# Seven down products summed in three pairs of PSUM banks, and two token tiles stored from GpSimd's queue

## The chip, the cores and the metric

One core of one Trainium2 chip runs the kernel. The metric is the device time of one execution in microseconds; the kernel before took 1035.12 us, the median of three runs (1033.83 to 1036.23).

## The reference, cut to what matters

One decoder layer on 512 tokens of width 1024: two token mixers, a layer norm, a gated feed-forward part, and a second layer norm whose result is the output. Only the last step is touched here:

```python
def swiglu(x, w_gate, w_up, w_down):
    return (jax.nn.silu(x @ w_gate) * (x @ w_up)) @ w_down
...
ff = swiglu(h, w_ffn_gate[l], w_ffn_up[l], w_ffn_down[l])
h = layer_norm(DEEPNORM_ALPHA * h + ff, ln2_g[l], ln2_b[l])
```

All of it is float32. `w_down` is 2816 x 1024.

## The kernel before, in words

**The down product.** The product of the 512 x 2816 activations with the 2816 x 1024 weights is made with seven products of half-size blocks in place of eight (Winograd's form of Strassen's scheme): tokens in two halves of 256, the inner dimension in two halves of 1408 (11 blocks of 128), the columns in two halves of 512. Their left sides are the activation blocks `a11`, `a12`, `a22` and the combinations `s1` to `s4`, which VectorE (DVE) forms while the feed-forward products run; their right sides are `w_down`'s own blocks or combinations of them that were written to the DRAM buffer `td` earlier, through GpSimd's (POOL's) DMA queue (`combine_weights`, L1085 to L1097).

**One product** (loop at L1207). It walks six weight blocks (five of 128 x 1024 values, one of 128 x 512). For each, `load_w` (L164) issues a load on SyncE's (SP's) queue into one of three buffers `wr`; `split_w` (L173) makes a high part `wh` by a cast on ScalarE (ACT, L135) and a low part `wl` by a subtraction on DVE (L121), each with three buffers; `mm3` (L154) then issues three matmuls (high x high, high x low, low x high) for each 128 rows. The load goes on when the subtraction of three blocks earlier has freed its `wr`. While product q runs, `left` (L1173) splits the left side of product q+1 in the same way, on ACT and DVE. One product is 11 blocks x 2 token tiles (`i` = 0, 1) x 3 = 66 matmuls of 512 columns.

**Where results gather.** Each half product sits in a PSUM bank of 128 x 512. Once a product is complete, `Norm.add` (L992) adds the bank to the rows `h1` in SBUF on DVE: a scalar_tensor_tensor (L124), and, where the sum of that half row is then complete, a bn_stats (L998). In the kernel before, three pairs of banks take the products as: `c11` a11 then a12 on top; `cx` s2 then s3 on top; `cy` s1 then s4 on top; a22 has banks of its own (`dl`). The product a11 belongs to three sums of four, so `first_sum` reads its bank three times for each token tile. Names in the trace: `dc` is c11, `dx` is cx, `dy` is cy.

**The last product, a22** (`final`), keeps the split weights of blocks 3 to 5 in buffers of their own, runs all of token tile 2 through before tile 3 for them, and cuts tile 3's 512 columns into two groups of 256.

**The layer norm and the stores.** `Norm.finish` (L1000) makes mean and scale from the statistics in eight small DVE instructions and one ACT square root. For tiles 0, 1 and 2 the row is then scaled on ACT and multiplied and added to on POOL (four instructions of 128 x 512 a tile); for tile 3 (`fast`) two DVE instructions a half do all. Tiles 0 and 1 are finished behind s4, the fifth product; tiles 2 and 3 behind a22, the seventh. Each finished tile is stored in two halves of 256 KB by DMAs that are issued from SP's queue:

```python
if last and (final or name == "s4"):
    t = i if name == "s4" else 2 + i
    lns[t].finish(t == 3)
    for jj in range(2):
        nc.sync.dma_start(out=out[0, t * P:(t + 1) * P, T * jj:T * jj + T], in_=h1[t][:, jj])
```

**What sets the order.** TensorE's (PE's) instructions run in the order of the program text. The other engines and queues are put in order by the scheduler at build time; each then runs its own list strictly in that order, so an instruction that waits holds those behind it on the same engine or queue.

Of the kernel before, what the change touches and what calls it, by code (L numbers as in the profile page):

```python
# [30 lines left out]
ALPHA = 2.0 ** 0.25  # L31
LN_EPS = 1e-5
RMS_EPS = 1e-6
P = 128
T = 512
# [11 lines left out]
def layer_kernel(  # L47
# [7 lines left out]
    nc = tc.nc  # L55
    ctx.enter_context(tc.manual_schedule(engines={mybir.EngineType.PE}))
    V, S, G, PE = nc.vector, nc.scalar, nc.gpsimd, nc.tensor
# [13 lines left out]
    def slot(name, dt=F32):  # L71
        if not line:
            raise RuntimeError(f"no slot for {name}")
        tag = line.pop(0)
        t = big.tile([P, 2, T], dt, tag=tag, name=name)
        held[id(t)] = (t, tag)
        return t

    def free(*tiles):
        for t in tiles:  # L80
            line.append(held.pop(id(t))[1])
# [3 lines left out]
    def bank(ring, name):  # L85
        tag = rings[ring].pop(0)
        rings[ring].append(tag)
        return pp.tile([P, T], F32, tag=tag, name=name)

    def bankp(name):  # L90
        return bank("p", name)

    def bankd(name):
        return bank("d", name)
# [19 lines left out]
    def flat(t):  # L114
        return t.rearrange("p a b -> p (a b)")
# [38 lines left out]
    def mm3(ps, wh, wl, rh, rl, start, stop, **kw):  # L154
        PE.matmul(ps, wh, rh, start=start, stop=False, **kw)  # L155
        PE.matmul(ps, wh, rl, start=False, stop=False, **kw)  # L156
        PE.matmul(ps, wl, rh, start=False, stop=stop, **kw)  # L157
# [6 lines left out]
    def load_w(src, raw=None):  # L164

        wcount[0] += 1
        if raw is None:
            raw = wp.tile([P, 1024], F32, tag="wr", bufs=3, name=f"wr{wcount[0]}")
        v = view_w(raw, *src.shape[1:])
        nc.sync.dma_start(out=v, in_=src)  # L170
        return v

    def split_w(raw, eng=None, hi=None, lo=None):  # L173

        wcount[0] += 1
        if hi is None:
            hi = wp.tile([P, 1024], F32R, tag="wh", name=f"wh{wcount[0]}")
        if lo is None:
            lo = wp.tile([P, 1024], F32R, tag="wl", name=f"wl{wcount[0]}")
        n = raw.shape[1] * raw.shape[2]  # L180
        split_flat(hi[:, :n], lo[:, :n], raw.rearrange("p a b -> p (a b)"), eng)
        return view_w(hi, *raw.shape[1:]), view_w(lo, *raw.shape[1:])
# [211 lines left out]
    for b in range(4):  # L394
        G.tensor_copy(out=eye32[32 * b:32 * b + 32],
                      in_=ident[32 * b:32 * b + 32, 32 * b:32 * b + 32])
# [474 lines left out]
    for n in range(4 * NK):  # L871

        k, i = (n // 4, n % 4) if n < 24 else (6 + n % 2, (n - 24) // 2)
# [150 lines left out]
    h1 = []  # L1024
    for i in range(4):
        t = slot(f"h1{i}")
# [4 lines left out]
    lns = [Norm(h1[i], g1, b1, f"ln1{i}") for i in range(4)]  # L1031
# [23 lines left out]
    for i in range(4):  # L1055
        ps = bankp(f"mx1_{i}")
# [22 lines left out]
    a11 = []  # L1079
# [83 lines left out]
    lns = [Norm(h1[i], g2, b2, f"ln2{i}", 4 if i == 3 else 2) for i in range(4)]  # L1163

    def rows_of_weights(i, c):
        return lambda p, n: wd[:, 2 * p + i:2 * p + i + 2 * n - 1:2, T * c:T * c + T]

    def combined(c):
        return lambda p, n: td[p:p + n, :, T * c:T * c + T].rearrange("k p c -> p k c")
# [3 lines left out]
    def left(n, p, m):  # L1173

        t = slot(f"{n}{p}", F32R)
        split(t[:, 0, 0:256 * m], t[:, 1, 0:256 * m], flat(parts[n][p // 4])[:, 256 * (p % 4):256 * (p % 4 + m)])
        if p % 4 == 2 or p + m == NP:
            free(parts[n][p // 4])
        return t

    c11 = [bankp(f"dc{i}") for i in range(2)]
    cx = [bankp(f"dx{i}") for i in range(2)]
    cy = [bankd(f"dy{i}") for i in range(2)]

    def first_sum(i, ps):
        for ln, c in ((lns[i], T), (lns[2 + i], 0), (lns[2 + i], T)):
            ln.add(ps, c, last=False)

    def onto(lo, i0, **kw):
        return lambda i, ps: lns[i0 + i].add(ps, lo, **kw)  # L1190

    def p7_done(i, ps):
        lns[2 + i].add(ps, T, 1.0)
        lns[2 + i].add(ps, 0, 1.0, False)


    products = [
        ("a11", rows_of_weights(0, 0), c11, True, first_sum),
        ("s2", combined(3), cx, True, onto(T, 0, alpha=1.0, last=False)),
        ("s1", combined(0), cy, True, onto(T, 2, alpha=1.0, last=False)),  # L1200
        ("a12", rows_of_weights(1, 0), c11, False, onto(0, 0)),
        ("s4", rows_of_weights(1, 1), cy, False, onto(T, 0, alpha=1.0)),
        ("s3", combined(1), cx, False, p7_done),
        ("a22", combined(2), None, True, onto(0, 2, alpha=1.0)),
    ]
    ready = a11
    for q, (name, right, banks, new, then) in enumerate(products):  # L1207
        lhs, ready = ready, []
        final = q == 6
        tops = [[(0, b)] for b in banks] if not final else [  # L1210
            [(0, bankp("dl0"))], [(0, bankp("dl1")[:, 0:256]), (256, bankd("dl2")[:, 0:256])]]
        pend = []
        for m, (p, n) in enumerate(blocks):
            keep = final and m >= 3
            extra = [flat(slot(f"wd{m}{e}", F32R)) if keep else None for e in range(2)]
            pend.append((m, n, *split_w(load_w(right(p, n)), None, *extra)))
            if not final:
                ready.append(left(products[q + 1][0], p, n))
            if keep and m < 5:
                continue  # L1220
            last = m == len(blocks) - 1
            for i in range(2):
                for c, ps in tops[i]:
                    w = ps.shape[1]
                    for mm, nn, wh, wl in pend:
                        for k in range(nn):
                            ts = slice(256 * k + P * i, 256 * k + P * i + P)
                            mm3(ps, lhs[mm][:, 0, ts], lhs[mm][:, 1, ts], wh[:, k, c:c + w], wl[:, k, c:c + w],
                                new and mm == k == 0, last and mm == m and k == nn - 1,
                                **({} if new else dict(skip_group_check=True)))  # L1230
                    if last:
                        if final:
                            lns[2 + i].add(ps, c, 1.0)
                        else:
                            then(i, ps)
                if last and (final or name == "s4"):
                    t = i if name == "s4" else 2 + i
                    lns[t].finish(t == 3)
                    for jj in range(2):
                        nc.sync.dma_start(out=out[0, t * P:(t + 1) * P, T * jj:T * jj + T], in_=h1[t][:, jj])  # L1240
            pend = []
        free(*lhs)

# [23 lines left out]
```

## Time and profile before

| | us |
|---|---|
| median of three runs | 1035.12 |
| the profiled execution | 1030.49 |
| its span, first to last instruction | 1028.8 |
| around the span | 1.7 |
| PE busy | 987.4 |
| DVE busy | 622.8 |
| ACT busy | 453.2 |
| POOL busy | 274.3 |

The span is what the rows below divide; times in them are microseconds from its start. The seven products take its last eighth, from 898.6 on. A busy PE is not a PE at its peak, since its clock can be granted at half; the row of the granted clock says when. Idle time before an instruction stands in brackets in a timeline, with what ended it.

### The profile page before, as it was taken

The numbers are of one execution on the slowest core, as the hardware profiler recorded it, in microseconds if no ns is written. First come the engines' busy times: TensorE is split into PE (matmuls) and PEld (weight loads), VectorE is DVE, ScalarE is ACT, GpSimd is POOL, SyncE is SP. The second block draws the span as 40 slices with busy tenths as digits, with TensorE's granted clock in tenths as the row PEclk, the third lists the DMA queues.
The fourth block names the chain that finished last, engine by engine and source line by source line (L and its number), as shares of the span: only waits on it lengthen the run. The fifth ranks groups of instructions, "written<-read, shape, count | busy, mean of one in ns | idle before, by whom it ended". The sixth has DMA issues, their size and how long they took to land.

```text
span 1028.8 us, 14366 instructions
## 1 busy us (share of the span) xinstructions
PE 987.4 (96%) x5531; PEld 811.6 (79%) x5531; DVE 622.8 (61%) x1321; ACT 453.2 (44%) x621; POOL 274.3 (27%) x278
## 2 busy tenths in 40 slices
PE   7999989999999999999999999999999999999974
PEld 4887767877887888788888888898788888878864
DVE  3769989837777872264333555957543334597565
ACT  5589463368326643764311333322222222465432
POOL 2372624516332723274100003232100000000052
PEclk9999999999999999999999999999999999999996
DMA  8332223223222323153334337489833333346551
GB/s 252 108 99 55 80 73 83 63 72 82 63 62 73 90 65 92 42 145 111 102 97 151 101 122 207 178 298 376 283 92 103 103 92 113 103 143 204 195 162 64
DMA packets 161544, 128.52 MB, mean 125 GB/s; under 512 B 5499, under 2 KB 140860, under 8 KB 161476
## 3 DMA queue, kind: packets, MB, share of 16 engines
q1 hardware_dynamic: 152608, 100.17, 33.1%
q0 software_dynamic: 7552, 27.27, 7.3%
q8 instruction: 43, 0.70, 0.3%
q10 hardware_dynamic: 1316, 0.16, 0.1%
q14 instruction: 25, 0.20, 0.1%
HBM read 113.94 MB, written 13.65 MB: 124 GB/s over the span
## 4 chain that ended last, share of the span: by engine, by line
PE 56%; issue 16%; DVE 14%; DMA 5%; ACT 4%; POOL 4%; SPq 0%; DVEq 0%; ACTq 0%; POOLq 0%
PE pj L155 3%; DMA b<-in_w_ffn_down 3%; PE pj L157 3%; PE pj L156 3%; PE g L155 3%; PE g L157 3%; PE g L156 3%; DVE xa L121 3%; PE fu L155 2%; PE fu L156 2%; PE fu L157 2%; PE fg L157 2%; PE fg L155 2%; PE fg L156 2%; PE yl L157 2%
## 5 line engine op out<-in xcount | busy, mean ns | idle before, releaser
L135 ACT CAST wh<-wr 128x1024 fp32r<-128x1024 f32 (+1 forms) x163 | 168.5, 1034 | 374.2 <-PE fg L156 78.0
L121 POOL TENSOR_TENSOR wl<-wr,wh 128x512 fp32r<-128x512 f32 x128 | 172.6, 1371 | 216.2 <-ACT wh L135 212.9
L121 DVE TENSOR_TENSOR wl<-wr,wh 128x1024 fp32r<-128x1024 f32 x99 | 117.9, 1193 | 131.9 <-ACT wh L135 131.8
L155 PE MATMUL pj<-xT,wh 128*128 128x512 f32 x224 | 92.6, 413 | 0.0
L157 PE MATMUL pj<-xT,wl 128*128 128x512 f32 x224 | 88.0, 393 | 0.0
L156 PE MATMUL pj<-xT,wh 128*128 128x512 f32 x224 | 87.9, 392 | 0.0
L127 ACT ACT_TABLE_LOAD x62 | 79.5, 1283 | 12.8 <-DMA rw<-in_lru_conv_w 7.2
L157 PE MATMUL fg<-hk,wl 128*128 128x512 f32 x160 | 62.4, 390 | 0.5 <-DVE wl L121 0.5
L155 PE MATMUL fg<-hk,wh 128*128 128x512 f32 x160 | 62.3, 389 | 0.0
L156 PE MATMUL fg<-hk,wh 128*128 128x512 f32 x160 | 62.3, 389 | 0.0
L155 PE MATMUL fu<-hk,wh 128*128 128x512 f32 x160 | 62.2, 389 | 0.0
L156 PE MATMUL fu<-hk,wh 128*128 128x512 f32 x160 | 62.2, 389 | 0.0
L157 PE MATMUL fu<-hk,wl 128*128 128x512 f32 x160 | 62.2, 389 | 0.0
L155 PE MATMUL g<-xT,wh 128*128 128x512 f32 x128 | 51.1, 399 | 0.0
L124 DVE SCALAR_TENSOR_TENSOR x<-pj,cols,x 128x511 f32<-128x511 f32 (+2 forms) x60 | 44.5, 742 | 9.7 <-ACT x L127 9.3
L157 PE MATMUL g<-xT,wl 128*128 128x512 f32 x128 | 50.0, 391 | 0.0
L156 PE MATMUL g<-xT,wh 128*128 128x512 f32 x128 | 49.9, 390 | 0.0
L157 PEld LDWEIGHTS pj<-xT,wl 128*128 128x128 f32 x224 | 42.3, 189 | 9.2
L155 PEld LDWEIGHTS pj<-xT,wh 128*128 128x128 f32 x224 | 42.5, 190 | 7.9
L121 POOL TENSOR_TENSOR h<-h,g 128x512 f32<-128x512 f32 x6 | 10.0, 1664 | 145.4 <-ACT h L127 145.4
L156 PEld LDWEIGHTS pj<-xT,wh 128*128 128x128 f32 x224 | 42.6, 190 | 7.3
L121 DVE TENSOR_TENSOR xa<-xa 128x16 f32<-128x16 f32 (+14 forms) x116 | 37.6, 324 | 2.3
(380 smaller groups left out, 2370.6 us busy)
## 6 DMA issues: line engine op xcount, KB each, us to landing
wr<-in_w_in SPq DMA_DIRECT2D x64, 512.0 KB, 3.7
wr<-in_w_ffn_gate SPq DMA_DIRECT2D x22, 512.0 KB, 3.6
wr<-in_w_ffn_up SPq DMA_DIRECT2D x22, 512.0 KB, 3.6
b<-in_w_ffn_down POOLq DMA_DIRECT2D x22, 512.0 KB, 5.8
td<-b POOLq DMA_DIRECT2D x22, 512.0 KB, 4.6
wr<-td SPq DMA_DIRECT2D x20, 512.0 KB, 3.9
wr<-in_w_ffn_down SPq DMA_DIRECT2D x15, 512.0 KB, 3.3
wr<-in_w_branch_lru SPq DMA_DIRECT2D x8, 512.0 KB, 3.5
```

What stands on the lines that cost most here:

```text
L121: return eng.tensor_tensor(out=o, in0=a, in1=b, op=op)
L124: return V.scalar_tensor_tensor(out=o, in0=a, scalar=s, in1=b, op0=op0, op1=op1)
L127: return S.activation(out=o, in_=i, func=func, **kw)
L135: S.copy(out=hi, in_=src)
L155: PE.matmul(ps, wh, rh, start=start, stop=False, **kw)
L156: PE.matmul(ps, wh, rl, start=False, stop=False, **kw)
L157: PE.matmul(ps, wl, rh, start=False, stop=stop, **kw)
```

## The change

Three pairs of banks are kept, now `ca`, `cb`, `cc`. a11, s2, s3 and, for the first token tile, a22 are gathered one on top of the other in `ca`, which is read in between (after a11 for columns 0 to 511 of tiles 0 and 1, after s2 for columns 512 to 1023 of these, after s3 for tiles 2 and 3); s1 and s4 share `cb`; a12 has `cc`. The order of s1 and s2, and that of s3 and s4, are exchanged, so s4, behind which tiles 0 and 1 are finished, is now the sixth product and not the fifth. The stores of tiles 0 and 1 are issued from POOL's queue; those of tiles 2 and 3 stay on SP's.

```diff
@@ -1178,37 +1178,37 @@
             free(parts[n][p // 4])
         return t
 
-    c11 = [bankp(f"dc{i}") for i in range(2)]
-    cx = [bankp(f"dx{i}") for i in range(2)]
-    cy = [bankd(f"dy{i}") for i in range(2)]
-
-    def first_sum(i, ps):
-        for ln, c in ((lns[i], T), (lns[2 + i], 0), (lns[2 + i], T)):
-            ln.add(ps, c, last=False)
+
+    ca = [bankp(f"da{i}") for i in range(2)]
+    cb = [bankd(f"db{i}") for i in range(2)]
+    cc = [bankp(f"dc{i}") for i in range(2)]
 
     def onto(lo, i0, **kw):
         return lambda i, ps: lns[i0 + i].add(ps, lo, **kw)
 
     def p7_done(i, ps):
         lns[2 + i].add(ps, T, 1.0)
-        lns[2 + i].add(ps, 0, 1.0, False)
+        if i == 1:
+            lns[3].add(ps, 0, last=False)
 
 
     products = [
-        ("a11", rows_of_weights(0, 0), c11, True, first_sum),
-        ("s2", combined(3), cx, True, onto(T, 0, alpha=1.0, last=False)),
-        ("s1", combined(0), cy, True, onto(T, 2, alpha=1.0, last=False)),
-        ("a12", rows_of_weights(1, 0), c11, False, onto(0, 0)),
-        ("s4", rows_of_weights(1, 1), cy, False, onto(T, 0, alpha=1.0)),
-        ("s3", combined(1), cx, False, p7_done),
-        ("a22", combined(2), None, True, onto(0, 2, alpha=1.0)),
+        ("a11", rows_of_weights(0, 0), ca, True, onto(0, 0, last=False)),
+        ("s1", combined(0), cb, True, onto(T, 2, last=False)),
+        ("s2", combined(3), ca, False, onto(T, 0, last=False)),
+        ("a12", rows_of_weights(1, 0), cc, True, onto(0, 0, alpha=1.0)),
+        ("s3", combined(1), ca, False, p7_done),
+        ("s4", rows_of_weights(1, 1), cb, False, onto(T, 0, alpha=1.0)),
+        ("a22", combined(2), ca, False, None),
     ]
     ready = a11
     for q, (name, right, banks, new, then) in enumerate(products):
         lhs, ready = ready, []
         final = q == 6
-        tops = [[(0, b)] for b in banks] if not final else [
-            [(0, bankp("dl0"))], [(0, bankp("dl1")[:, 0:256]), (256, bankd("dl2")[:, 0:256])]]
+        tops = [[(0, b, new)] for b in banks]
+        if final:
+
+            tops[1] = [(0, bankd("dl1")[:, 0:256], True), (256, bankd("dl2")[:, 0:256], True)]
         pend = []
         for m, (p, n) in enumerate(blocks):
             keep = final and m >= 3
@@ -1220,24 +1220,25 @@
                 continue
             last = m == len(blocks) - 1
             for i in range(2):
-                for c, ps in tops[i]:
+                for c, ps, fresh in tops[i]:
                     w = ps.shape[1]
                     for mm, nn, wh, wl in pend:
                         for k in range(nn):
                             ts = slice(256 * k + P * i, 256 * k + P * i + P)
                             mm3(ps, lhs[mm][:, 0, ts], lhs[mm][:, 1, ts], wh[:, k, c:c + w], wl[:, k, c:c + w],
-                                new and mm == k == 0, last and mm == m and k == nn - 1,
-                                **({} if new else dict(skip_group_check=True)))
+                                fresh and mm == k == 0, last and mm == m and k == nn - 1,
+                                **({} if fresh else dict(skip_group_check=True)))
                     if last:
                         if final:
-                            lns[2 + i].add(ps, c, 1.0)
+                            lns[2 + i].add(ps, c, 1.0 if i else ALPHA)
                         else:
                             then(i, ps)
                 if last and (final or name == "s4"):
                     t = i if name == "s4" else 2 + i
                     lns[t].finish(t == 3)
                     for jj in range(2):
-                        nc.sync.dma_start(out=out[0, t * P:(t + 1) * P, T * jj:T * jj + T], in_=h1[t][:, jj])
+                        (nc.sync if final else G).dma_start(out=out[0, t * P:(t + 1) * P, T * jj:T * jj + T],
+                                                            in_=h1[t][:, jj])
             pend = []
         free(*lhs)
```

## Rows read from the trace of the kernel before

**Rows 1.** The page: busy time, share of the span, instructions
```profile
PE 987.4 (96%) x5531; PEld 811.6 (79%) x5531; DVE 622.8 (61%) x1321; ACT 453.2 (44%) x621; POOL 274.3 (27%) x278
```

**Rows 2.** Busy time by stretch: sixth product, seventh, the slow part of that
```profile
core 0: us, PE busy (x) PEld busy (x) DVE busy (x) ACT busy (x) POOL busy (x), PEclk, DMA share, GB/s
975.90:990.90 15.00, 15.00 (x67) 12.41 (x67) 12.41 (x25) 10.31 (x13) 7.48 (x5) 1.00 0.55 183
990.90:1017.10 26.20, 18.42 (x99) 15.69 (x97) 11.85 (x26) 4.38 (x6) 5.46 (x4) 0.87 0.30 91
...
1005.00:1009.60 4.60, 4.38 (x15) 3.92 (x16) 3.16 (x4) 1.74 (x3) 0.00 (x0) 0.51 0.22 59
```

**Rows 3.** Timeline of PE: start, duration, instruction [idle before, what ended it]
```profile
898.58 0.39 PE L155 MATMUL dc<-wh,a 128*128 128x512 f32 x1
...
918.70 0.50 PE L156 MATMUL dx<-wl,s 128*128 128x512 f32 x1 [2.05 <-DVE wl L121]
...
975.73 0.39 PE L155 MATMUL dx<-wh,s 128*128 128x512 f32 x1
...
990.69 0.39 PE L155 MATMUL dl<-wh,a 128*128 128x512 f32 x1
...
995.43 0.50 PE L156 MATMUL dl<-wl,a 128*128 128x512 f32 x1 [1.56 <-DVE wl L121]
...
1003.96 0.80 PE L155 MATMUL dl<-wh,a 128*128 128x512 f32 x1 [5.67 <-ACT wh L135]
...
1013.26 0.28 PE L155 MATMUL dl<-wd,a 128*128 128x256 f32 x1
...
1016.73 0.28 PE L157 MATMUL dl<-wd,a 128*128 128x256 f32 x1
```

**Rows 4.** Timeline of SP's queue, then its waits (us in total, times, longest)
```profile
966.19 17.91 SPq L170 DMA_DIRECT2D wr<-td  x8
986.27 10.61 SPq L1240 DMA_DIRECT2D out<-h  x4
996.98 8.55 SPq L170 DMA_DIRECT2D wr<-td  x4
...
SPq L1240 <- POOL h L121: 28.8, 6, 14.9
```

**Rows 5.** Timeline of DVE, around the second product's start and at 986
```profile
913.71 3.80 DVE L124 SCALAR_TENSOR_TENSOR h<-h,dc 128x512 f32<-128x512 f32 x8
917.43 3.49 DVE L121 TENSOR_TENSOR wl<-wr,wh 128x1024 fp32r<-128x1024 f32 x3
...
986.18 0.68 DVE L121 TENSOR_TENSOR wl<-wr,wh 128x512 fp32r<-128x512 f32 x1
```

**Rows 6.** Groups by form, 898 to 1029: one read of a full bank
```profile
L124 DVE SCALAR_TENSOR_TENSOR h<-h,dc 128x512 f32<-128x512 f32 x6 | 3.8, 681 | 1.1 <-PE dc L157 1.1
```

**Rows 7.** Timeline of POOL: tiles 0 and 1 (first, slowest, last), then tile 2
```profile
983.26 1.61 POOL L121 TENSOR_TENSOR h<-h,g 128x512 f32<-128x512 f32 x1 [124.32 <-ACT h L127]
...
989.35 2.28 POOL L121 TENSOR_TENSOR h<-h,g 128x512 f32<-128x512 f32 x1
...
994.33 2.19 POOL L121 TENSOR_TENSOR h<-h,b 128x512 f32<-128x512 f32 x1
1017.57 1.27 POOL L121 TENSOR_TENSOR h<-h,g 128x512 f32<-128x512 f32 x1 [21.05 <-ACT h L127]
...
1022.25 1.26 POOL L121 TENSOR_TENSOR h<-h,b 128x512 f32<-128x512 f32 x1
```

**Rows 8.** Groups of POOL by line: DMA issues, count, busy, mean ns
```profile
L1096 POOL DMA_DIRECT2D td<-b x22 | 11.8, 536 | 50.5 <-DVE b L121 38.5 <-DVE hk L121 11.0 <-PE f L157 0.9
```

**Rows 9.** DMA issues: count, KB each, median us from issue to landing
```profile
td<-b POOLq DMA_DIRECT2D x22, 512.0 KB, 4.6
...
out<-h SPq DMA_DIRECT2D x8, 256.0 KB, 2.3
```

**Rows 10.** Timeline of SP's queue: the last store
```profile
1024.75 0.33 SPq L1240 DMA_DIRECT2D out<-h  x1
```

## What the change does to the time: a prediction

> **What bounds the kernel now.** I read the page first: PE is busy for 96% of the span [rows 1], so time can come only from places where PE stands still or runs slowly, and from the end behind its last matmul. Next comes the table of stretches over the seven products. The sixth product takes 15.0 us at a granted clock of 1.00; the seventh, a22, with as many multiplications, takes 26.2 us, and DVE, ACT and POOL are all less than half busy in it [rows 2]. So none of them is short of time there: something is late.
>
> The timeline of PE says what. One product takes 990.69 - 975.73 = 14.96 us, which is 66 matmuls at 0.2267 us. In a22, PE stands for 1.56 us and then for 5.67 us [rows 3], and after the long stop its granted clock is 0.51, the 1.2 GHz level, from 1005.0 to 1009.6 [rows 2]. The 256-column matmuls follow each other every 0.12 us (29 steps from 1013.26 to 1016.73 [rows 3]). An unhindered a22 has 33 matmuls of 512 columns and 66 of 256, 33 x 0.2267 + 66 x 0.12 = 15.4 us, so 10.9 us are lost there.
>
> SP's queue gives the cause. Eight loads (six of s3, two of a22) are issued, then come the four stores of tiles 0 and 1, from 986.27 to 996.88, and only behind them a22's other four loads, at 996.98 [rows 4]. The stores wait for POOL's layer norm (14.9 us in the longest wait [rows 4]), which works from 983.26 to 996.52 [rows 7]. The buffer for the first held load was free at 986.86, when the low part of the block before was done [rows 5]: the queue and not the buffer held it, for 10 us.
>
> The other places: PE stood 2.05 us at the second product [rows 3], since DVE made 3.80 us of bank reads (`first_sum`) before the three low parts that were due [rows 5]. And 11.8 us lie between PE's last matmul (1016.73 + 0.28 = 1017.0) and the end: the layer norms of tiles 2 and 3, and the last stores.
>
> **The change, part by part.**
>
> *Stores of tiles 0 and 1 leave SP's queue.* Nothing that waits for POOL now stands ahead of a22's loads. These go back to waiting for their buffers, as the loads of the sixth product did, which ran without a stop [rows 2]. Taken: the whole 10.9 us. The other end is that the last blocks are wanted sooner (below, the third rival).
>
> *The reads.* Counting a full bank as one, twenty reads become fifteen: after a11 two in place of six, after s3 three in place of four. At 0.68 us each [rows 6] this is 3.4 us of DVE, beside PE's work except at the second product. There 3.80 - 2 x 0.68 = 2.4 us go from in front of the due low parts, more than the 2.05 us stall: PE gains 2.05 us, at the least 0, if another piece of work is put in the gap.
>
> *Waits that the banks add.* s2 may write `ca` only after a11's reads, s3 after s2's, a22 after s3's: a whole other product of 14.96 us lies between each pair, so they cost nothing; without it PE would stand for the two reads, 1.4 us. One is closer. The ring `d` has three banks left, so the second half of tile 3 in a22 writes the bank of `cb` that s4's read leaves. That read is due some 0.7 us before a22 starts (tile 0's matmuls end three before s4's last), and the matmuls that want it come 6 x 0.2267 + 6 x 0.12 = 2.1 us after the start. Taken: nothing; at most the 1.56 us of the stall now seen at that place.
>
> *s4 becomes the sixth product.* PE's own timeline: 898.58 + 6 x 14.96 = 988.34 for the end of s4, and 988.34 + 15.4 + 0.16 = 1003.9 for PE's last matmul to end, 13.1 us sooner than 1017.0. If the 11.8 us behind it stayed, the span would be 1015.7.
>
> They do not stay. Tiles 0 and 1 are now finished during a22, and POOL does this and then tile 2. In the kernel before, POOL's first instruction starts 983.26 - 975.73 = 7.53 us behind s4 [rows 3, 7], and its eight take 13.26 us; tile 2's four, much later, take 5.94 us [rows 7]. Now POOL starts at 988.34 + 7.53 = 995.9 and is not done with tiles 0 and 1 when tile 2 is ready: tile 2's rows reach POOL in the kernel before 1017.57 - 1013.26 = 4.3 us behind the last of its matmuls [rows 3, 7], now at 988.34 + 11.8 + 4.3 = 1004.4. Behind POOL's instructions for tiles 0 and 1 stand the moved stores as well.
>
> *The four stores on POOL's queue.* The nearest rows are the stores to `td` from the same queue, 0.536 us of POOL each [rows 8], so 2.1 us. At the other end they cost POOL what the slowest instruction beside DVE was stretched by, 2.28 - 1.26 = 1.0 us each more [rows 7], 6.2 us in all. I take 2.1, since the rows are of the same operation. Landing takes 4.6 us for twice the bytes there, against 2.3 on SP's queue [rows 9]; tile 1's stores go out 5.5 us or more before tile 2 is done, which covers it.
>
> *The sum.* POOL's instructions of 128 x 512 take 1.26 us alone and up to 2.28 us while DVE works [rows 7]. Tiles 0 and 1: 8 x 1.27 = 10.2 to 13.26 us; tile 2: 5.1 to 5.94. DVE has fewer low parts to make during a22's second half and is done near 1011.6, so I take the middle of each: 12.5 + 2.1 + 5.5 = 20.1 us from 995.9, POOL done at 1016.0. Behind it three stores go from SP's queue, 0.33 us each, and from the end of the last of them to the end of the span it is 1028.8 - 1025.08 = 3.7 us [rows 10]: 4.7 us together. Span 1020.7, so 8.1 us less than 1028.8. By the ends of these terms POOL is done between 1013.3 and 1017.2, or 1.56 us later with the stall above: 5.3 to 10.8 us less. (With the stores at 6.2 us as well, every term at its worst, it would be 1.2 us less.)
>
> The profiled execution took 1030.49 us, 1.69 around its span, and lies 4.6 below the median of 1035.12. I put the difference on the median: 1035.12 - 8.1 = 1027.0, own range 1024.3 to 1029.8.
>
> **The rivals.**
>
> *POOL keeps up.* If tiles 0 and 1 are done before tile 2 arrives, DVE's tile 3 sets the end: span 1015.7, time 1022.0. For it: PE's gain of 13.1 us is real. Against it: POOL would have to be done with all twelve instructions and four stores by 1015.7 - 4.7 = 1011.0, 15.1 us after it starts, where the quickest rows give 10.2 + 2.1 + 5.1 = 17.4. Only an earlier start, or POOL's list in another order, does it.
>
> *The stores are held while DVE works.* Then tile 1's two stores go out only as DVE ends, 7.7 us behind PE's last matmul [rows 3, 10], at 1011.6; two stores and tile 2 follow, 1.1 + 5.5, and the 4.7: span 1022.9, time 1029.2. Against it, 22 stores were issued from POOL at a mean of 0.536 us [rows 8] while DVE was forming the combinations that they store. The Trainium skill ("SBUF — State Buffer", "SBUF: two separate sides") names this as a trap: a DMA from GpSimd's queue needs its descriptors written by GpSimd, which certain two-port DVE instructions lock out, and it advises SP's or ACT's queue, which speaks against this change; the rows of 0.536 us do not show it, and no row tells whether DVE's instructions behind a22 are of that kind. By the figures of the page's next section ("A bandwidth-pool intuition that's wrong"), 3.1 us in place of 0.62 for a DMA, four stores would add 4 x 2.5 = 9.9 us, an estimate from that page, and the time would be 1036.9.
>
> *a22 still starves.* PE takes blocks 3 to 5 of tile 2 in a row (6 x 0.2267 = 1.4 us each), and those of tile 3 after them, so block 4 is wanted 1.4 us and block 5 2.8 us sooner than with tile by tile in turn, while DVE and ACT make the layer norm of tiles 0 and 1 in between. For it: low parts behind bank reads stopped PE for 1.56 us. Against it: the same mix ran in the sixth product without a stop [rows 2]. If all 10.9 us are lost again, PE ends at 1014.8, the span is 1026.6 and the time 1032.9.
>
> *POOL is slow throughout (slower than before).* The place is the same row of twelve instructions. If each takes the slowest row's 2.28 us with 0.07 between, they and the stores take 30.3 us: POOL done at 1026.2, span 1030.9, time 1037.2. It decides against the change from a mean of 2.1 us on. For it: two of the eight now seen took 2.19 and 2.28 us [rows 7]. Against it: the eight have a mean of 13.26 / 8 = 1.66, and DVE has nothing left to do for tile 2's four.
>
> **How the numbers follow.** About 0.2%, 2.1 us, is what a measurement of this kernel can tell from no change. POOL sets the end as in the sum: 0.68, time 1027.0. POOL keeps up: 0.12. Stores held: 0.08. a22 starves: 0.07, a little over half of it faster by more than 0.2%, the rest not. POOL slow throughout: 0.05, slower. Faster 0.68 + 0.12 + 0.08 + 0.04 = 0.92, same 0.03, slower 0.05. The range runs from the first rival's 1022.0 to 1031.0: it holds the sum's own range, the held stores and part of the starved cases, and leaves out the slow POOL and what lies beyond either end.
>
> **What would show it right or wrong.** Right: a22's loads follow s4's on SP's queue with no store between; a22 takes PE 15 to 17 us at a clock of 1.00; no 2 us stop at the second product; PE's last matmul near 1004; POOL without a pause from about 996 to 1016, its stores at 0.5 us; 16 to 18 us behind PE's last matmul in place of 11.8. Wrong: POOL waiting for tile 2 (first rival), stores of over 1 us on POOL or a pause in front of them (second), PE stops or a clock near 0.5 in a22 (third), POOL's instructions at a mean over 2 us (fourth).

## The result and the profile after

The changed kernel takes 1025.76 us, the median of five runs (1023.59 to 1028.68), against 1033.83 us for the kernel before in its five (1031.51 to 1036.23). The ratio is 0.9925, with a 95% interval of 0.9897 to 0.9952: 0.75% faster, clear of noise. The profiled execution took 1025.76 us with a span of 1024.0.

The first view is the timeline of PE in the changed kernel: the first matmul of a11, of the second product, of a22, and the last one.

```profile
902.31 0.39 PE L155 MATMUL da<-wh,a 128*128 128x512 f32 x1
...
917.27 0.39 PE L155 MATMUL db<-wh,s 128*128 128x512 f32 x1
...
992.07 0.39 PE L155 MATMUL da<-wh,a 128*128 128x512 f32 x1
...
1007.41 0.28 PE L157 MATMUL dl<-wd,a 128*128 128x256 f32 x1
```

Six products take 992.07 - 902.31 = 89.76 us, which is 6 x 14.96: there is no stop in them, where [rows 3] show one of 2.05 us. The table of stretches says the same of the sixth product and of a22, which takes 15.6 us at a clock of 1.00, against 26.2 at 0.87 [rows 2] with the stops of 1.56 and 5.67 us [rows 3]. Its third line is what lies behind PE's last matmul, now 16.3 us:

```profile
977.10:992.10 15.00, 15.00 (x68) 12.41 (x67) 9.85 (x15) 5.90 (x6) 0.00 (x0) 1.00 0.60 198
992.10:1007.70 15.60, 15.59 (x100) 14.02 (x98) 13.52 (x34) 8.51 (x12) 8.02 (x7) 1.00 0.28 94
1007.70:1024.00 16.30, 0.00 (x0) 0.00 (x0) 11.76 (x13) 1.72 (x3) 10.20 (x10) 0.57 0.29 113
```

On SP's queue the six loads of a22 follow s4's, and only the stores of tiles 2 and 3 come behind:

```profile
967.58 14.96 SPq L170 DMA_DIRECT2D wr<-in_w_ffn_down  x6
983.33 12.85 SPq L170 DMA_DIRECT2D wr<-td  x6
1015.89 4.10 SPq L1240 DMA_DIRECT2D out<-h  x4
```

POOL's timeline, which answers to [rows 7], is one line from 999.59 to 1018.42, the stores among it, with no pause but one of 0.30 us:

```profile
999.59 1.37 POOL L121 TENSOR_TENSOR h<-h,g 128x512 f32<-128x512 f32 x1 [136.91 <-ACT h L127]
...
1007.13 0.58 POOL L1240 DMA_DIRECT2D out<-h  x1
1007.74 1.27 POOL L121 TENSOR_TENSOR h<-h,b 128x512 f32<-128x512 f32 x1
1008.96 1.27 POOL L121 TENSOR_TENSOR h<-h,g 128x512 f32<-128x512 f32 x1
1010.16 0.58 POOL L1240 DMA_DIRECT2D out<-h  x1
...
1012.34 0.56 POOL L1240 DMA_DIRECT2D out<-h  x1 [0.30 <-POOL h L121]
1012.91 1.27 POOL L121 TENSOR_TENSOR h<-h,g 128x512 f32<-128x512 f32 x1
...
1017.16 1.26 POOL L121 TENSOR_TENSOR h<-h,b 128x512 f32<-128x512 f32 x1
```

DVE in the same time, in its timeline, works on tiles 2 and 3. One instruction on 128 x 1 values, the last small one of tile 2, takes 2.80 us there, where its like took 0.16 us a step before:

```profile
1007.26 0.16 DVE L124 SCALAR_TENSOR_TENSOR ln_rs<-ln_w,ln_rs 128x1 f32<-128x1 f32 x1
1007.45 2.80 DVE L124 SCALAR_TENSOR_TENSOR ln_w<-ln_mv,ln_rs 128x1 f32<-128x1 f32 x1
...
1012.52 0.15 DVE L1005 RECIPROCAL ln_rs<-ln_va 128x1 f32<-128x1 f32 x1
...
1014.67 1.21 DVE L124 SCALAR_TENSOR_TENSOR ln_w<-ln_rs,ln_xh 128x1 f32<-128x1 f32 x1
...
1017.13 2.50 DVE L124 SCALAR_TENSOR_TENSOR h<-h,ln_rs,b 128x512 f32<-128x512 f32 x2
```

It ends at 1010.25, just as POOL goes from two instructions on SBUF to a store (1010.16). DVE ends at 1019.63, 1.2 us behind POOL, and the last store and the end follow. The chain of work that ended last is on DVE all the way from tile 2's last matmul; no instruction of POOL is on it. Its first step and its last two:

```profile
1004.13 0.70 DVE h L124
...
1017.13 1.83 DVE h L124
1018.97 0.66 DVEq L1264
```

**How the runs are compared.** In this execution a11 began at 902.31, and at 898.58 in the one before [rows 3]. Most of these 3.7 us is one stop at 732.38, in the feed-forward part, where both kernels have the same instructions in the same order; the same matmul stood for 0.54 us in the kernel before. The first line is from the changed kernel, the second from the one before:

```profile
732.38 0.50 PE L157 MATMUL fg<-hk,wl 128*128 128x512 f32 x1 [2.87 <-DVE wl L121]
```

```profile
730.26 0.50 PE L157 MATMUL fg<-hk,wl 128*128 128x512 f32 x1 [0.54 <-DVE wl L121]
```

The start of a11 moved between 898.7 and 904.3 over all the runs below. So beside the ratio the text gives S, from a11's first matmul to the end of the span, in the profiled execution: 1028.8 - 898.58 = 130.2 us before, 1024.0 - 902.31 = 121.7 after, 8.5 us less. S comes from one execution of each kernel, so differences of half a microsecond in it say nothing; the ratio comes from all executions.

### The profile page after: what moved, and what is told of

Same layout as the page of the kernel before. It is cut to its first block, busy times and chain, and to the rows that moved or that the text cites. A ratio compares the mean times of both kernels' runs of the same rounds, so it can differ in the third digit from the quotient of the medians.

```text
span 1024.0 us, 14357 instructions
## 1 busy us (share of the span) xinstructions
PE 986.0 (96%) x5531; PEld 811.1 (79%) x5531; DVE 623.0 (61%) x1314; ACT 453.2 (44%) x621; POOL 273.2 (27%) x282
## 4 chain that ended last, share of the span: by engine, by line
PE 68%; DVE 15%; ACT 5%; DMA 5%; issue 4%; POOL 2%; ACTq 0%; DVEq 0%; POOLq 0%; SPq 0%
DMA b<-in_w_ffn_down 3%; PE g L155 3%; PE pj L155 3%; PE g L157 3%; PE g L156 3%; PE fu L157 3%; PE fu L155 3%; PE fu L156 3%; DVE xa L121 3%; PE fg L157 3%; PE fg L155 3%; PE pj L157 3%; PE pj L156 3%; PE fg L156 3%; ACT L127 2%
## 5 line engine op out<-in xcount | busy, mean ns | idle before, releaser
L127 ACT ACT_TABLE_LOAD x62 | 79.5, 1283 | 12.5 <-DMA rw<-in_lru_conv_w 7.2
```

The source lines that it names most:

```text
L127: return S.activation(out=o, in_=i, func=func, **kw)
```

## The experiments

The change has three parts: three pairs of banks with fewer reads, s4 as the sixth product, and the moved stores. The exchange of s1 and s2 goes with the banks in every run and was not tried alone; nor was the late s4 with old banks and POOL's queue. What the runs gave, with all three parts together in the second line:

| run | banks and reads | s4 | stores 0, 1 | S, us | ratio (95%) |
|---|---|---|---|---|---|
| before | old | 5th | SP | 130.2 | 1 |
| changed | new | 6th | POOL | 121.7 | 0.9925 (0.9897 to 0.9952) |
| queue alone | old | 5th | POOL | 125.4 | 0.9938 (0.9921 to 0.9956) |
| late s4 alone | old | 6th | SP | 123.7 | 0.9950 (0.9932 to 0.9968) |
| reads alone | new | 5th | SP | 127.4 | 0.9977 (0.9964 to 0.9991) |
| reads and late s4 | new | 6th | SP | 119.6 | 0.9893 (0.9875 to 0.9912) |
| reads and queue | new | 5th | POOL | 121.5 | 0.9911 (0.9891 to 0.9930) |

**The queue alone.** The kernel before, with

```diff
-                        nc.sync.dma_start(out=out[0, t * P:(t + 1) * P, T * jj:T * jj + T], in_=h1[t][:, jj])
+                        (nc.sync if final else G).dma_start(out=out[0, t * P:(t + 1) * P, T * jj:T * jj + T], in_=h1[t][:, jj])
```

> The kernel before with one edit: the stores of tiles 0 and 1 go through POOL's queue; banks, reads and the order of the products stay. S is the stretch from the first matmul of a11 to the end of the span: 130.2 us in the kernel before, 121.7 in the changed one. Theory (the stores on SP's queue held a22's loads, and in the changed kernel POOL's line of twelve instructions and four stores sets the end): a22 runs at full clock, the 2.05 us stop at the second product and at most the 1.56 us one stay, POOL is done with tiles 0 and 1 before tile 2 comes, the tail stays 11.8: S 119.3 to 120.9, so this one edit gives all of the gain or a little more, ratio about 0.990. Rival (banks and order give the gain): a22 still stops for over 4 us, S 126 or more, ratio 0.995 to 1.0.

Measured: S 125.4, ratio 0.9938. Both missed. The loads were free, but a22 still stopped for 1.18 and 2.25 us, each time for a low part. DVE's timeline shows the first of these stretched from 1.22 to 3.42 us (beside a POOL without stores, in the kernel before, it took 1.68), and POOL's beside it that this ends 1.14 us after a store begins:

```profile
991.23 3.42 DVE L121 TENSOR_TENSOR wl<-wr,wh 128x1024 fp32r<-128x1024 f32 x1 [1.93 <-ACT wh L135]
```

```profile
991.02 1.30 POOL L121 TENSOR_TENSOR h<-h,b 128x512 f32<-128x512 f32 x1
992.27 1.29 POOL L121 TENSOR_TENSOR h<-h,g 128x512 f32<-128x512 f32 x1
993.51 0.58 POOL L1240 DMA_DIRECT2D out<-h  x1
```

So with s4 fifth, POOL works on tiles 0 and 1 just where a22's first low parts are due, and DVE stands meanwhile; the last run below takes POOL's work away there. The second low part comes behind the four reads of s3 as well. In this execution the granted clock then fell to half, and PE's last matmul ended 113.2 us behind a11's first, 2.4 us later than the stops explain. The run with fresh banks below has the same two stops at a clock of 1.00, so the S of this run holds some 2 us that its stops alone need not cost (columns as in [rows 2]):

```profile
1002.00:1004.00 2.00, 2.00 (x10) 2.00 (x10) 0.26 (x1) 0.00 (x0) 0.00 (x0) 0.50 0.80 231
```

**All stores on SP's queue, the rest changed.**

```diff
-                        (nc.sync if final else G).dma_start(out=out[0, t * P:(t + 1) * P, T * jj:T * jj + T],
+                        nc.sync.dma_start(out=out[0, t * P:(t + 1) * P, T * jj:T * jj + T],
```

> The changed kernel with the stores of tiles 0 and 1 back on SP's queue; banks, reads and order as changed. Theory: with s4 sixth the scheduler puts all six loads of a22 ahead of these stores, so nothing is held; POOL is rid of four issues of 0.58 us, and its line ends 2.3 us sooner: S 119.4, ratio 0.990. Rival 1 (the queue gives the gain): a22's loads are held again, S 126 to 130, ratio 0.997 or more. Rival 2 (DVE's work for tile 3 sets the end, not POOL's line): S 121.7 as in the changed kernel, ratio 0.9925.

Measured: S 119.6, ratio 0.9893, as the theory had it. SP's timeline shows that the scheduler puts the stores behind all of a22's loads by itself, so nothing is held:

```profile
981.30 12.85 SPq L170 DMA_DIRECT2D wr<-td  x6
1000.33 15.82 SPq L1240 DMA_DIRECT2D out<-h  x8
```

Once s4 is late and the banks are new, the move to POOL's queue costs 2.1 us of S. The intervals of 0.9893 and 0.9925 overlap a little, so a run below doubles the number of stores.

**s4 fifth again, with the changed banks.**

```diff
-        ("s3", combined(1), ca, False, p7_done),
         ("s4", rows_of_weights(1, 1), cb, False, onto(T, 0, alpha=1.0)),
-        ("a22", combined(2), ca, False, None),
+        ("s3", combined(1), ca, False, p7_done),
+        ("a22", combined(2), ca, True, None),
...
+            tops[0] = [(0, bankp("dl0"), True)]
```

and the read of columns 0 to 511 in `p7_done` for both tiles, with the factor of a22's sum for tile 2 back at 1.0.

> The changed kernel with s4 fifth and s3 sixth again, a22 in banks of its own, and the read of columns 0 to 511 after s3 for both tiles; stores of tiles 0 and 1 on POOL's queue. Theory: no stop of PE, and POOL done with tiles 0 and 1 before tile 2 comes: S = 6 x 14.96 + 15.6 + 11.8 = 117.2, ratio 0.987 to 0.989. Rival (the late order costs nothing): S 121.7, ratio 0.9925.

Measured: S 122.0, ratio 0.9909 (0.9889 to 0.9930). A miss, partly of the experiment: the ring `p` has four banks, so `dl0` is the bank of `ca` that s3's reads were due in, and PE stood 2.69 us for them. With free banks instead (`dl0` from ring `d`, `dl2` from `cc`'s first bank):

> The run with s4 fifth again, now with banks for a22 that nobody reads any more (before, its first bank was the one that s3's reads were due in: PE stood 2.69 us there). Stores of tiles 0 and 1 on POOL's queue. Theory (POOL's instructions hold the SBUF port that DVE's subtractions need: one took 3.42 us in place of 1.22 in the run with the queue alone): a low part of a22's first blocks is late again, PE stands 1 to 3 us and may lose clock: S 118.7 to 121, ratio 0.988 to 0.991. Rival (the shared bank was all that was wrong): S 117.2, ratio 0.987 or less.

Measured: S 121.5, ratio 0.9911 (0.9891 to 0.9930). PE no longer stands for the bank, but for low parts, 1.18 and 2.25 us, as in the run with the queue alone; S is 0.5 us over the theory's range and far from the rival's 117.2.

```profile
990.04 0.50 PE L156 MATMUL dl<-wl,a 128*128 128x512 f32 x1 [1.18 <-DVE wl L121]
...
995.38 0.50 PE L156 MATMUL dl<-wl,a 128*128 128x512 f32 x1 [2.25 <-DVE wl L121]
```

**The same with all stores on SP's queue**, so that only banks and reads differ from the kernel before:

> The same kernel (three pairs of banks, fewer reads, s4 fifth, a22 in banks of its own) with all stores on SP's queue: banks and reads without the late order and without the queue. Theory: the stop at the second product goes (2 us), but four of a22's loads stand behind the stores of tiles 0 and 1 again and a22 loses about what it lost before: S 127 to 128.5, ratio 0.997 to 0.999. Rival (the reads matter more than that, since the bank reads in front of a22's low parts were part of its stop): S 122 to 125, ratio 0.992 to 0.995.

Measured: S 127.4, ratio 0.9977, as expected. Four of a22's loads stand behind the stores on SP's queue again, and PE stops for 5.12 us. The first low part of a22 takes 1.68 us here and 3.41 us in the run just above, which differs in nothing but the queue of the four stores.

```profile
984.46 10.61 SPq L1240 DMA_DIRECT2D out<-h  x4
995.17 7.98 SPq L170 DMA_DIRECT2D wr<-td  x4
```

```profile
986.99 1.68 DVE L121 TENSOR_TENSOR wl<-wr,wh 128x1024 fp32r<-128x1024 f32 x1 [1.94 <-ACT wh L135]
```

**Late s4 alone.** The kernel before, with

```diff
-        ("s4", rows_of_weights(1, 1), cy, False, onto(T, 0, alpha=1.0)),
         ("s3", combined(1), cx, False, p7_done),
+        ("s4", rows_of_weights(1, 1), cy, False, onto(T, 0, alpha=1.0)),
```

> The kernel before with one edit: s3 and s4 exchanged, so s4 is the sixth product. Banks and reads as before, all stores on SP's queue. S as before (first matmul of a11 to the end of the span): 130.2 in the kernel before, 121.7 in the changed one, 119.6 in the changed one with all stores on SP's queue. Theory (the late s4 alone frees a22's loads): the stop of 2.05 us at the second product stays, a22 runs in some 15.6 us, the tail is POOL's line as in the changed kernel without POOL's stores, 14.2: S about 121.9, ratio 0.990 to 0.992. Rival (banks or queue are needed for it): S 126 or more, ratio 0.996 or more.

Measured: S 123.7, ratio 0.9950 (0.9932 to 0.9968). SP's timeline shows all of a22's loads issued with no store ahead of them, so the late s4 alone frees them and the mechanism of the rival is out:

```profile
987.05 14.01 SPq L170 DMA_DIRECT2D wr<-td  x6
1007.22 15.82 SPq L1240 DMA_DIRECT2D out<-h  x8
```

But S is 1.8 us above the theory, and the ratio lies between the two ranges, its interval reaching into the rival's. Of the 1.8 us, 1.46 are a stop that the theory did not have: s3's four reads with their statistics, 3.8 us in one piece, stand in front of three low parts on DVE, now that s4 comes behind s3:

```profile
979.76 1.28 DVE L124 SCALAR_TENSOR_TENSOR h<-h,dx 128x512 f32<-128x512 f32 x2 [1.09 <-PE dx L157]
980.97 0.69 DVE L998 BATCH_NORM_STATS2 ln_st<-h 128x6 f32<-128x512 f32 x1
...
983.54 3.49 DVE L121 TENSOR_TENSOR wl<-wr,wh 128x1024 fp32r<-128x1024 f32 x3
```

```profile
984.81 0.50 PE L156 MATMUL dy<-wl,s 128*128 128x512 f32 x1 [1.46 <-DVE wl L121]
```

With the changed banks there are three reads, and a low part of 1.22 us gets in between. So, in S of one execution each, the new banks and fewer reads are worth 123.7 - 119.6 = 4.1 us where s4 is late, against 2.8 where it is early.

**The layer norm without POOL.** The changed kernel, with

```diff
-                    lns[t].finish(t == 3)
+                    lns[t].finish(True)
```

> The changed kernel with the layer norm of all four tiles in its DVE form (two instructions a half on DVE; POOL and ACT do none of the scaling). POOL is left with the four stores. Theory (POOL's line sets the end, and its instructions stretch DVE's): PE's last matmul at 105.4 behind a11's first as now, DVE's instructions at 0.74 us and its small ones at 0.2 us again: S 114 to 117, ratio 0.985 to 0.988. Rival (the amount of DVE's work sets the end): twelve instructions of 0.74 us more on DVE, of which four lie behind PE's end: S 124 or more, ratio 0.995.

Measured: S 115.9, ratio 0.9858 (0.9839 to 0.9876), as the theory had it. The edit takes ACT's scaling of these tiles away along with POOL's work. DVE has more to do and is done sooner, 112.9 us behind a11's first matmul in place of 117.3: in tile 3's part of its timeline the large instructions take 0.74 us and the small ones 0.2 again.

```profile
1009.80 0.74 DVE L124 SCALAR_TENSOR_TENSOR h<-h,ln_mv,g 128x512 f32<-128x512 f32 x1
...
1011.24 0.21 DVE L124 SCALAR_TENSOR_TENSOR ln_w<-ln_rs,ln_xh 128x1 f32<-128x1 f32 x1
1011.49 0.16 DVE L124 SCALAR_TENSOR_TENSOR ln_rs<-ln_w,ln_rs 128x1 f32<-128x1 f32 x1
1011.68 1.42 DVE L124 SCALAR_TENSOR_TENSOR h<-h,ln_rs,b 128x512 f32<-128x512 f32 x2
```

The same with all stores on SP's queue:

> The changed kernel with the layer norm of all tiles on DVE (S 115.8, ratio 0.9858 with tiles 0 and 1 stored from POOL's queue), and all stores on SP's queue. Theory (a store on POOL's queue costs only what it takes of a POOL that is the bound): POOL does nothing here, so S 115.8 within 0.5, ratio 0.9845 to 0.987. Rival (the issue on POOL is dear in itself): S lower by 1 us or more, ratio 0.984 or less.

Measured: S 115.8, ratio 0.9861 (0.9842 to 0.9880), no difference: the four stores on POOL's queue cost nothing that can be seen here, where POOL has nothing else to do. These two, 1017.8 and 1017.3 us, are the fastest versions found.

**Tile 2 alone moved to DVE**, stores on SP's queue (`finish(t >= 2)`):

> The changed kernel with all stores on SP's queue and tile 2's layer norm in the DVE form, tiles 0 and 1 still on POOL. S as before: 119.6 with all stores on SP's queue, 115.8 with all four tiles' norm on DVE. Theory (the end is POOL's line, and DVE is held by POOL's instructions only while these run): POOL is done 108.3 us behind a11's first matmul, PE's last matmul at 105.4; DVE then does tile 2 and tile 3 unhindered: S 115.5 to 117.5, ratio 0.985 to 0.988. Rival (DVE's amount of work sets the end): S 119 or more.

Measured: S 118.4, ratio 0.9870 (0.9848 to 0.9892): 0.9 us above the range of S, inside that of the ratio. POOL was done at 1009.55, 109.1 us behind a11, and until then DVE's large instructions of the layer norm took 1.4 to 1.6 us, its small ones up to 1.2; from 1009.8 on they took 0.74 and 0.2. This is one execution and one engine doing the same steps twice, with and without POOL beside it:

```profile
1005.46 1.63 DVE L124 SCALAR_TENSOR_TENSOR h<-h,ln_mv,g 128x512 f32<-128x512 f32 x1
...
1013.08 0.74 DVE L124 SCALAR_TENSOR_TENSOR h<-h,ln_mv,g 128x512 f32<-128x512 f32 x1
```

**Eight stores in place of four on POOL's queue.** The changed kernel, with tiles 0 and 1 stored in pieces of 256 columns:

```diff
-                    for jj in range(2):
-                        (nc.sync if final else G).dma_start(out=out[0, t * P:(t + 1) * P, T * jj:T * jj + T],
-                                                            in_=h1[t][:, jj])
+                    n = T if final else T // 2
+                    for c in range(0, D, n):
+                        (nc.sync if final else G).dma_start(out=out[0, t * P:(t + 1) * P, c:c + n],
+                                                            in_=h1[t][:, c // T, c % T:c % T + n])
```

> The changed kernel with each store of tiles 0 and 1 cut in two, so POOL issues eight stores of 128 KB in place of four of 256 KB. Theory (every issue takes 0.58 us of a POOL whose line sets the end): S 121.7 + 4 x 0.58 = 124.0, ratio 0.994 to 0.996. Rival (stores are off the path, and the difference to the run with all stores on SP's queue is chance): S 121.7, ratio 0.9925.

Measured: S 124.2, ratio 0.9938 (0.9914 to 0.9962). S is as the theory had it; the ratio lies just below its range, and its interval holds the rival's 0.9925 too. With no store, four and eight on POOL's queue POOL's line lasts 17.0, 18.8 and 21.0 us and S is 119.6, 121.7 and 124.2, some 0.58 us a store; the ratios 0.9893, 0.9925 and 0.9938 go the same way, with intervals that overlap from step to step. The intervals of none and eight are apart.

**s4 fifth and no layer norm on POOL.** The run with fresh banks, with `finish(True)` for all tiles:

> s4 fifth, a22 in banks of its own, the layer norm of all tiles on DVE, stores of tiles 0 and 1 on POOL's queue, where nothing else is. Theory (in the runs with s4 fifth it was POOL's instructions that stretched the low parts): the low parts take 1.22 us again, PE stops at most 1.5 us behind the four reads after s3, tiles 0 and 1 are done before a22, so the tail is shorter by what they took there: S 114.5 to 116.5, ratio 0.984 to 0.987. Rival (the early s4 is slow whatever POOL does): a22 stops for 3 us or more, S 118 or more, ratio 0.989 or more.

Measured: S 116.4, ratio 0.9871 (0.9845 to 0.9896). The low parts take 1.22 us, and one stop of 1.42 us is left, behind the four reads. So it was POOL's instructions that stretched the first low part. Without them no difference between the early and the late s4 can be told (116.4 and 115.9); nor can one with them and with the same queue (121.5 and 121.7).

```profile
992.53 1.22 DVE L121 TENSOR_TENSOR wl<-wr,wh 128x1024 fp32r<-128x1024 f32 x1
```

## Why the prediction was right, and where it was not

The time lay in the range, 1.2 us from the forecast. The whole of that is the kernel before, which came out at 1033.83 us this time and not at 1035.12: the forecast gain of 8.1 us was measured as 1033.83 - 1025.76 = 8.07. In S the sum gave 1020.7 - 898.6 = 122.1 against 121.7. So close a hit is in part luck, since two terms were off and cancelled, and one step had the wrong cause. Its steps:

- **a22 gets its 10.9 us back, and the second product its 2.05.** Right to 0.1 us: 15.6 us for a22, 105.4 us from a11's first matmul to the end of PE's work (1007.69 - 902.31), where 6 x 14.96 + 15.6 = 105.4 was forecast. PE's last matmul ended at 1007.7 and not at 1003.9 for what lies ahead of a11.
- **Whose doing it is: wrong.** The step "Stores of tiles 0 and 1 leave SP's queue" was given the whole 10.9 us. In the changed order these stores would have come behind a22's loads on SP's queue too, and with them there the kernel is faster, S 119.6. What frees the loads in the changed kernel is s4 in sixth place. The move of the stores brought time where s4 was fifth (5.9 us between 127.4 and 121.5, 4.8 between 130.2 and 125.4) and cost some where it was sixth.
- **The reads.** The 2.05 us were right, but not that this was all: three reads in place of four also spare a stop behind s3, which the runs with four reads there show (1.46 us with late s4 and old banks, 1.42 in the last run). That the ring `d` has three banks left was wrong (it has four); no number hung on it here.
- **POOL's line.** It starts 999.59 - 992.07 = 7.5 us behind s4's end, as forecast, and lasts 18.8 us for 20.1: the eight instructions of tiles 0 and 1 took 1.37 us on average where 12.5 / 8 = 1.56 was put in, and the stores 0.58 where 0.536 was (2.3 us for 2.1). The prediction called 12.5 the middle of 10.2 and 13.26, but the middle is 11.7; with it the line would have been 19.3 us.
- **The end.** Here a step failed. "DVE ... is done near 1011.6" left out that a POOL that never pauses holds DVE. DVE was done at 1019.63, 117.3 us behind a11's first matmul, where the forecast is 1011.6 - 898.6 = 113.0. It came 1.2 us behind POOL, so the chain that ends last is DVE's, slowed by POOL, and not POOL's line as such; 5.6 us follow POOL's last instruction in place of 4.7. The trace of before already had 1028.8 - 1023.51 = 5.3 us there [rows 7], with DVE's last instruction 1.2 us behind POOL's. The two misses, in POOL's line and behind it, nearly cancel. That POOL's instructions are the cause, and not the amount of DVE's work, is shown by taking them away (S 115.9), by the same DVE instructions with and without POOL beside them in the run with tile 2 on DVE (1.63 and 0.74 us), and by adding four stores between them (124.2).
- **The rivals.** Held stores: every one took 0.56 to 0.58 us while DVE worked, so the trap that the Trainium skill describes ("SBUF — State Buffer", "SBUF: two separate sides") did not show; no row tells whether any of DVE's instructions here was of the kind it names. The other way round did: POOL held DVE. The same section of the Trainium skill says that a GpSimd instruction and a DVE instruction with two SBUF inputs exclude each other when the first reads SBUF, and that the one that starts second is blocked while the other runs. The rows agree that DVE is blocked: 2.80 us for a 128 x 1 instruction here, 5.52 us for one in the run with eight stores, and 3.42 us for a low part; that these waits outlast one POOL instruction is taken up in the last section. POOL keeping up, starving and a slow POOL did not happen.

## What to carry to other kernels

A queue that runs strictly in order, as SP's does here, can be relieved in two ways: take the waiting transfer off it, or make the work it waits for come later than everything that would stand behind it. The two overlap, and the first can cost where the second has already been done (2.1 us of S here); look at the order on the queue as the scheduler makes it before crediting either. GpSimd's elementwise work beside VectorE's was not free here, even where VectorE waits for none of its results: the same layer norm was 3.8 us quicker in S on VectorE alone (115.8 against 119.6, both with all stores on SP's queue; the intervals of the ratios, 0.9861 and 0.9893, touch), and 5.8 us with the stores on GpSimd's queue (115.9 against 121.7, intervals apart).

## What was not expected of the hardware

A DVE instruction that is held by POOL can wait over several POOL instructions, not one: 2.80, 3.42 and 5.52 us, of which 0.16, 1.22 and 0.16 are its own, against POOL instructions of 1.27 us. In the run with eight stores it is freed as POOL begins to issue stores; it began to stand while POOL was still issuing the three stores before:

```profile
1004.99 5.52 DVE L124 SCALAR_TENSOR_TENSOR ln_rs<-ln_w,ln_rs 128x1 f32<-128x1 f32 x1
```

```profile
1003.92 1.64 POOL L1241 DMA_DIRECT2D out<-h  x3
1005.57 2.49 POOL L121 TENSOR_TENSOR h<-h,g 128x512 f32<-128x512 f32 x2
1008.01 2.48 POOL L121 TENSOR_TENSOR h<-h,b 128x512 f32<-128x512 f32 x2
1010.43 2.19 POOL L1241 DMA_DIRECT2D out<-h  x4
```

In these rows only DVE instructions with two inputs in SBUF were held. In the changed kernel, from 1010 to POOL's end, those took 1.15 to 2.10 us, large and small alike, while a reciprocal of one input took 0.15, a bn_stats of 256 columns 0.43 and a read of 256 columns of a bank 0.41, beside the same POOL.

Why the same low part takes 1.68 us beside a POOL without stores and 3.41 us beside one with them stays open: the rows show that its place between POOL's instructions differs, not what decides who comes next.
